# A transformer block on one core: values of twelve heads by seven products of halves, ahead of the attention

## The chip, the core and the metric

The kernel runs on one core of a Trainium2 chip. The metric is the device time of one execution in microseconds (us): the median of the runs, 2047.81 us for the kernel before (three runs, 2047.67 to 2048.41).

## The reference

One residual block over 512 positions of width 2048, all in float32:

```python
h = rmsnorm(x, g_attn)
proj = h @ w_in                      # columns: qa ka va | qf kf vf | f (8 gates)
o_sb  = stick_breaking_attention(qa, ka, va)       # 8 heads of 128
log_f = log_sigmoid(f + b_f)
o_fox = forgetting_attention(qf, kf, vf, log_f)    # 8 heads; z + c[t] - c[s], c = cumsum(log_f)
x = x + concat(headnorm(o_sb), headnorm(o_fox)) @ w_out
u = relu(rmsnorm(x) @ w_up)
x = x + (u * u) @ w_down
y = rmsnorm(x)
```

The change touches the projection of the values (va, vf), the row of c that the forgetting heads add to their scores, the preparation of w_out, and the norm of a head's output.

## The kernel before

**Precision.** Each float32 operand is split into a high part (a cast to a rounded format, on ScalarE, L71 or L74) and a low part (the difference, on VectorE, L72 or L75). A product is three matmuls, high x high, high x low, low x high (`mm3`, L103 to L106). So every chunk of weights that comes in by DMA (`load_w`, L88, tile `wraw`, three buffers) costs a cast and a subtraction of its size before TensorE can use it (tiles `wh`, `wl`, three buffers, `hi_lo`, L80).

**Order.** Loops are unrolled, and a planner orders the instructions of each engine ahead of time, by program order as priority, by estimated durations and by free buffers; `tc.high_priority()` lifts the attention of a head above the rest, and `tc.issue_after(ins)` keeps instructions on the engine of `ins` behind it. Each engine then takes its own list strictly in that order; loads and stores go through SP's list.

**First stage** (L348 to L369). x arrives in blocks, is transposed on TensorE (L179), multiplied by g_attn and split into hH, hL (16 tiles of 128 x 512, kept until the last projection). In the same loop the values of the first pair of heads and the 8 gate columns (264 columns) are accumulated for four row blocks of 128 (`accumulate_v`, L182): the activations are the stationary operand, the weights move. The squares of x (L366, ScalarE) give the row factors r1 (`row_rstd`), which scale everything projected.

**Attention** (L450 to L475). Heads go in pairs, n = 0, 2, ... 14: the forgetting heads 6, 7, 0 to 5 first, then the eight stick-breaking heads. For a pair:

- `project` (L451) makes four projections q, k of 16 steps x 3 matmuls of 512 columns (accumulator `accq`), then `qf` (L221) and its split into u tiles, one buffer for each of the pair's four.
- For n < 8, two calls of `sums_of_weights` (L429): for one pair of row blocks of w_out, four differences of quarters (L439 to L442), splits of parts of them, and stores to DRAM (`wsums`, `whigh`, `wraws`), for seven products of halves in the output projection later.
- For n = 2, 6, 10, `accumulate_v` over 512 columns makes the values of four heads, this pair's and the next's: 16 steps x 4 row blocks x 3 matmuls (`accv`); n = 14 does 256 columns. `take_v` (L204) scales by r1 and splits into vh, vl.
- `attend_sb` (L288) or `attend_fox` (L304): scores, then exponentials, sums and masks on ScalarE, VectorE and POOL in the tile `w`, then `weigh` (L246): transposes of `w` (L251) into PSUM, split into `ph`, `pl`, matmuls with vh, vl into `o`, and the norm: squares (L277), their column sums by a matmul with ones (L282, L283), VectorE's mean plus epsilon (L284), logarithm and exponential (L110, L111), three VectorE steps (L112 to L114) and the scaled output in `mixed` (L286). `w`, `ph`, `pl` and the PSUM tile of scores have one buffer each, and the norm's intermediates live in `ph`, `pl`.
- A forgetting head gets its row of -c by a matmul of a selector with ckT (`ck`, L306), copied by ScalarE (`cb`, L308).

The rest, output projection and the two matrices of the MLP, already works with seven products of halves and is the same text after the change.

Of the kernel before, what the change touches and what calls it, by code (L numbers as in the profile page):

```python
# [8 lines left out]
F32 = mybir.dt.float32  # L9
# [17 lines left out]
NU = DFF // P // 2  # L27

# [7 lines left out]
def block_kernel(ctx, tc, x, g_attn, w_in, b_f, g_out_sb, g_out_fox, w_out, g_mlp, w_up, w_down, g_final, y):  # L36
# [10 lines left out]
    cp.tile([P, 96], F32, name="pad0")  # L47
    pad = ctx.enter_context(tc.tile_pool(name="pad", bufs=1, side="right"))
    pad.tile([P, 120], F32, name="pad2")
    mixp_cm = tc.tile_pool(name="mix", bufs=1, side="right", reuse_waits="tile")  # L50
    mixp = mixp_cm.__enter__()
    mixed = mixp.tile([P, 2 * NH, NT], F32, name="mixed")
    up_cm = tc.tile_pool(name="u", bufs=1, side="right", reuse_waits="tile")
    up = up_cm.__enter__()
# [70 lines left out]
    def along_free(trp, r, wide):  # L125

        for t in range(TB):
            dve.tensor_copy(wide[:, t * P:(t + 1) * P], r[:, t:t + 1].to_broadcast([P, P]))
        ps = trp.tile([P, NT], F32, tag="tr", name="trb")
        for t in range(TB):  # L130
            pe.transpose(ps[:, t * P:(t + 1) * P], wide[:, t * P:(t + 1) * P], ident)
        return ps
# [13 lines left out]
    cp.tile([P, 16], F32, name="pad1")  # L146
# [7 lines left out]
    wsums = dp.tile([P, NH // 2, 4, 2, 2, NT], F32, name="wsums")  # L154
    whigh = dp.tile([P, NH // 2, 2, NT], F32, name="whigh")
# [9 lines left out]

    with tc.tile_pool(name="att", bufs=1, side="right", reuse_waits="tile") as at:
# [3 lines left out]
        h4 = [[form1.tile([P, 4, NT], F32R, tag=EARLY[2 * i + j], name=f"h{c}{i}") for j, c in enumerate("HL")] for i in range(KC // 4)]  # L170
        hH, hL = ([h4[k // 4][c][:, k % 4, :] for k in range(KC)] for c in range(2))
        xq = x.rearrange("(t p) c -> p t c", p=P)

        def transpose_x(k, trp):

            c, i = divmod(k, 4)
            ps = trp.tile([P, NT], F32, tag="tr", name="tr")
            for t in range(TB):
                pe.transpose(ps[:, t * P:(t + 1) * P], mixed[:, 4 * c + t, i * P:(i + 1) * P], ident)  # L179
            return split(hH[k], hL[k], ps, g_in[:, k:k + 1])  # L180

        def accumulate_v(c0, m, steps, prepare=None, more=None, pool_=None):  # L182

            per = NT // m
            banks = [(acc if pool_ is None else pool_).tile([P, NT], F32, tag="acc", name="accv")
                     for _ in range(2 if more is not None else TB // per)]
            if more is not None:
                banks += [more.tile([P, NT], F32, tag="more", name="accm") for _ in range(2)]
            ps = [banks[t // per][:, t % per * m:(t % per + 1) * m] for t in range(TB)]
            k1 = 0  # L190
            for step in steps:
                k0, k1 = k1, k1 + step
                if prepare is not None:
                    prepare(k0, step)
                w = load_w([w_in[k0 * P:(k0 + step) * P, c:c + m // len(c0)].rearrange("(a p) c -> p a c", p=P) for c in c0],
                           step, m)
# [7 lines left out]
        def take_v(ps, pairs=1):  # L204
            vs = [tuple(at.tile([P, TB, 2 * P], F32R, tag=f"v{c}", name=f"v{c}", bufs=3) for c in "hl") for _ in range(pairs)]
            for t in range(TB):
                for i, (vh, vl) in enumerate(vs):
                    split(vh[:, t, :], vl[:, t, :], ps[t][:, i * 2 * P:(i + 1) * 2 * P], r1[:, t:t + 1])
                    last_heads[2] = lows[0]
            return vs  # L210

        def project_q(c0, c, rb):
# [8 lines left out]
            dve.tensor_tensor(f, ps, rb, op=ALU.mult)  # L221
# [24 lines left out]
        def weigh(h, v, hc, w, gv, left=2):  # L246
# [23 lines left out]
            if left == 1:  # L270
                n1 = at.tile([P, 2 * NT], F32, tag="vh", name="n1", bufs=3)
                n2 = at.tile([P, 2 * NT], F32R, tag="vl", name="n2", bufs=3)
# [11 lines left out]
            dve.tensor_scalar(va, q, 1.0 / P, EPS, op0=ALU.mult, op1=ALU.add)  # L284
            rsqrt(va, va, ra, sq)
# [18 lines left out]
        def attend_fox(h, v, hc, q, k):  # L304
            ck = atp.tile([P, NT], F32, tag="o", name="ck")
            pe.matmul(ck, nsel[:, h, :], ckT, start=True, stop=True)  # L306
            cb = at.tile([P, NT], F32, tag="ul5", name="cb")
            act.copy(cb, ck)  # L308
# [17 lines left out]
        o0 = 3 * WSB  # L326
        order = [NH + h for h in (6, 7, 0, 1, 2, 3, 4, 5)] + list(range(NH))

        def v_columns(h):
            return 2 * WSB + h * P if h < NH else o0 + 2 * WSB + (h - NH) * P  # L330

        with tc.tile_pool(name="tr0", bufs=2, space=PSUM) as trp:
            def columns(out, v, n):
                ps = trp.tile([P, NT], F32, tag="tr", name="trg")
                pe.transpose(ps[:, :n], v, ident[:n, :n])
                dve.tensor_copy(out, ps[:, :n])

            def column_vectors(out, *rows):
                n = sum(r.shape[0] for r in rows)
                v = at.tile([n, P], F32, tag="rows", name="rows")  # L340
                i = 0
                for r in rows:
                    act.dma_start(v[i:i + r.shape[0], :], r)
                    i += r.shape[0]
                columns(out, v, n)
# [1014 lines left out]
```

## Time and profile before

| | |
|---|---|
| median of three runs | 2047.81 us |
| span of the profiled execution, first to last instruction | 2045.7 us |
| instructions | 26813 |
| TensorE (PE) busy | 2030.4 us, 99% |
| VectorE (DVE) busy | 1666.6 us, 81% |
| ScalarE (ACT) busy | 1093.2 us, 53% |
| data moved by DMA | 402.40 MB, 197 GB/s |

The profile shows one execution; its own time outside the span is not listed, and the median of the runs is 2.1 us above the span. Engines: PE is TensorE's matmuls, PEld its weight loads, which overlap them; SP issues DMAs. L104 is line 104 of the kernel before. In a group's row, `out<-in` names the tiles, then come partitions x elements, the count, busy us and mean ns, and idle time ahead of it with what ended that. A timeline row has start, length, engine, line and tiles. A row of waits has the waiting group, what it waited for, us in total, times and the longest.

### The profile page before, as it was taken

What the parts mean: (1) busy time and instruction counts of PE and PEld (TensorE: products, weight loads), DVE (VectorE), ACT (ScalarE), POOL (GpSimd) and SP (SyncE); (2) the same over time, 40 slices, a digit from 0 to 9 for tenths busy, and PEclk for the clock granted to TensorE, in tenths of its full rate; (3) what the DMA queues carried; (4) which work ended last, traced back from release to release, by engine and by line L of the source; (5) the groups of instructions that cost most, each with busy time, mean ns of one, the idle gap of its engine ahead of it and who ended that gap; (6) DMA issues with size and microseconds to landing.
All of it is one profiled execution on the core that took longest, in us unless ns stands there. A gap on an engine that the chain in (4) does not pass through costs nothing.

```text
span 2045.7 us, 26813 instructions
## 1 busy us (share of the span) xinstructions
PE 2030.4 (99%) x10322; PEld 1734.8 (85%) x10322; DVE 1666.6 (81%) x1892; ACT 1093.2 (53%) x1578; POOL 57.5 (3%) x76
## 2 busy tenths in 40 slices
PE   9999999999999999999999999999999999999998
PEld 8888888888888888988888888888888888888887
DVE  5667755566577678899999999999799898898896
ACT  6434433445455566677677676776644434444344
POOL 0000000000010000000000000000000000000004
PEclk9999999999999999999999999999999999999999
DMA  7888743232328882656666667667685674674642
GB/s 249 295 284 271 251 131 86 73 93 75 80 74 276 283 275 91 219 175 193 210 193 215 196 198 220 188 208 257 223 296 211 218 253 178 235 253 172 224 160 87
DMA packets 258848, 402.40 MB, mean 197 GB/s; under 512 B 9456, under 2 KB 154912, under 8 KB 251168
## 3 DMA queue, kind: packets, MB, share of 16 engines
q1 hardware_dynamic: 257760, 398.56, 59.4%
q10 hardware_dynamic: 960, 2.13, 0.3%
q8 instruction: 81, 1.33, 0.3%
q14 instruction: 47, 0.39, 0.1%
HBM read 307.85 MB, written 92.80 MB: 196 GB/s over the span
## 4 chain that ended last, share of the span: by engine, by line
PE 94%; DVE 4%; ACT 1%; issue 1%; DMA 1%; POOL 0%; SPq 0%; ACTq 0%; DVEq 0%
PE psa L594 10%; PE accd L104 8%; PE accd L105 8%; PE accd L106 8%; PE accq L104 6%; PE accq L105 6%; PE accq L106 6%; PE psa L596 5%; PE psc L594 5%; PE psc L596 3%; PE psb L594 3%; PE accv L104 2%; PE accv L105 2%; PE accv L106 2%; PE m L104 1%; PE m L105 1%
## 5 line engine op out<-in xcount | busy, mean ns | idle before, releaser
L1172 ACT CAST wh<-wd 128x1024 fp32r<-128x1024 f32 x126 | 124.9, 999 | 167.7 <-PE accd L106 54.4
L1062 DVE TENSOR_TENSOR wl<-wu,wh 128x1024 fp32r<-128x1024 f32 x157 | 191.4, 1220 | 15.3 <-ACT wh L1056 15.3
L104 PE MATMUL accq<-hH,wh 128*128 128x512 f32 x512 | 200.4, 391 | 0.4 <-DVE vl L75 0.4
L105 PE MATMUL accq<-hL,wh 128*128 128x512 f32 x512 | 200.2, 391 | 0.0
L106 PE MATMUL accq<-hH,wl 128*128 128x512 f32 x512 | 200.2, 391 | 0.0
L594 PE MATMUL psa<-f,wh 128*128 128x512 f32 x728 | 182.4, 392 | 0.3 <-ACT l L628 0.3
L1056 ACT CAST wh<-wu 128x1024 fp32r<-128x1024 f32 x157 | 166.2, 1058 | 28.5 <-issue 11.3
L105 PE MATMUL accd<-wl,uf 128*128 128x512 f32 x436 | 169.6, 389 | 0.0
L106 PE MATMUL accd<-wh,uf 128*128 128x512 f32 x436 | 169.6, 389 | 0.0
L104 PE MATMUL accd<-wh,uf 128*128 128x512 f32 x436 | 169.5, 389 | 0.0
L72 DVE TENSOR_TENSOR wl<-wraw,wh 128x1024 fp32r<-128x1024 f32 (+2 forms) x101 | 119.0, 1179 | 57.8 <-ACT wh L71 52.2
L71 ACT CAST wh<-wraw 128x1024 fp32r<-128x1024 f32 (+2 forms) x101 | 101.8, 1009 | 111.6 <-PE accq L105 68.6
L1179 DVE TENSOR_TENSOR wl<-wd,wh 128x1024 fp32r<-128x1024 f32 x126 | 143.9, 1151 | 13.2 <-ACT wh L1172 12.7
L594 PEld LDWEIGHTS psa<-f,wh 128*128 128x128 f32 x728 | 131.0, 189 | 24.0 <-ACT l L628 0.5
L946 DVE TENSOR_TENSOR m<-m,accd 128x1024 f32<-128x1024 f32 x84 | 102.2, 1216 | 46.7 <-PE accd L106 46.7
L1172 ACT CAST wx<-wd 128x1024 fp32r<-128x1024 f32 (+1 forms) x82 | 80.8, 995 | 109.3 <-PE accd L106 43.0
L104 PEld LDWEIGHTS accq<-hH,wh 128*128 128x128 f32 x512 | 96.1, 188 | 20.2 <-PE accv L106 0.8
L106 PEld LDWEIGHTS accq<-hH,wl 128*128 128x128 f32 x512 | 96.2, 188 | 19.3
L105 PEld LDWEIGHTS accq<-hL,wh 128*128 128x128 f32 x512 | 96.2, 188 | 19.3
L104 PE MATMUL accd<-wx,uf 128*128 128x512 f32 x284 | 110.5, 389 | 0.0
L105 PE MATMUL accd<-wx,uf 128*128 128x512 f32 x284 | 110.5, 389 | 0.0
L106 PE MATMUL accd<-wx,uf 128*128 128x512 f32 x284 | 110.5, 389 | 0.0
(375 smaller groups left out, 4930.1 us busy)
## 6 DMA issues: line engine op xcount, KB each, us to landing
wu<-in_w_up_dram SPq DMA_DIRECT2D x60, 1024.0 KB, 6.6
ufd<-st SPq DMA_DIRECT2D x98, 512.0 KB, 4.1
wd<-in_w_down_dram SPq DMA_DIRECT2D x48, 1024.0 KB, 7.6
wraw<-in_w_in_dram SPq DMA_DIRECT2D x84, 512.0 KB, 3.8
uf<-ufd SPq DMA_DIRECT2D x42, 1024.0 KB, 7.2
mixed<-in_w_out_dram SPq DMA_DIRECT2D x8, 2048.0 KB, 7.7
wsums<-mixed SPq DMA_DIRECT2D x8, 2048.0 KB, 7.3
wo<-wsums SPq DMA_DIRECT2D x28, 512.0 KB, 5.0
```

Of the source, the lines that this page charges most:

```text
L71: ins = act.copy(hi, src)
L72: lows[0] = dve.tensor_tensor(lo, src, hi.bitcast(F32), op=ALU.subtract)
L104: pe.matmul(out, sh, mh, start=first, stop=False, skip_group_check=True)
L105: pe.matmul(out, sh, ml, start=False, stop=False, skip_group_check=True)
L106: return pe.matmul(out, sl, mh, start=False, stop=last, skip_group_check=True)
L594: pe.matmul(ps, hi[:, a, :], f_both(p, a), start=a == PAIRS[0] and p in (1, 5), stop=False, skip_group_check=True)
L596: ins = pe.matmul(ps[:, 2 * P:], lo[:, a, :], f_parts(p, a)[0], start=False, stop=a == PAIRS[-1], skip_group_check=True)
L946: dve.tensor_tensor(M[p][:, :, db, :], M[p][:, :, db, :], ps, op=ALU.add)
L1056: act.copy(rooms[k][0], srcs[k])
L1062: lows[0] = dve.tensor_tensor(lo, srcs.pop(k), hi.bitcast(F32), op=ALU.subtract)
L1172: act.copy(rooms[k + 3][0], srcs[k + 3])
L1179: dve.tensor_tensor(rooms[k + 2][1], srcs.pop(k + 2), rooms[k + 2][0].bitcast(F32), op=ALU.subtract)
```

## The change

1. **Values.** Before the attention, a stage of its own makes the values of the first seven pairs. The first pair and the gates are accumulated as before (with x's blocks k and k + 8 side by side). The other twelve heads are two groups of six (768 columns). For each group the activations (512 rows x 2048) and the weights (2048 x 768) are cut into halves both ways, and the four products of quarters, eight multiplications, become seven of sums and differences (the Winograd form): each 8 steps x 2 row blocks x 3 matmuls of 384 columns. The sums on the activations' side (x11, x21, x12, f5, and the splits in `make_left`) are made once, those on the weights' side per group, in place. Results are scaled by r1, added on VectorE, and stored to DRAM (`vd`); each pair loads its values back and splits them (`load_v`). The last pair is done as before.
2. **Sums of output weights.** One whole call per pair for n = 0 to 6; the other four are cut into halves of columns, three such pieces for each of n = 8, 10 and two for n = 12: seven pairs of heads instead of four.
3. **Gate rows.** c is transposed, negated, stored to DRAM (`ckd`), and each forgetting head loads its row broadcast over the partitions, instead of the selector matmul and the copy.
4. **Norm of a head.** The logarithm reads the sums from PSUM with scale and epsilon (a column `eps`); VectorE's step L284 goes, and L112 to L114 change their constants.
5. **Scale.** rbq, the row factors times 1/sqrt(128), goes; the query's multiply has the scale in it.

```diff
+        def v_product(p, b, ps, first):
+            b11, b12, b21, b22 = b
+            out, x_, y_ = {1: (b11, None, None), 2: (b21, None, None), 3: (b22, None, None), 5: (b11, b12, b11),
+                           6: (b11, b22, b11), 4: (b21, b21, b11), 7: (b12, b22, b12)}[p]
+            for a in range(0, K8, 2):
+                s_ = slice(a, a + 2)
+                if x_ is not None:
+                    dve.tensor_tensor(out[:, s_], x_[:, s_], y_[:, s_], op=ALU.subtract)
+                hi, lo = (w.rearrange("p (a b) -> p a b", a=2) for w in hi_lo(2 * NV))
+                split(hi, lo, out[:, s_])
+                for t in range(2):
+                    ts = slice(t * P, (t + 1) * P)
+                    for i in range(2):
+                        lh, ll = left(p, a + i)
+                        mm3(ps[t][:, :NV], lh[:, ts], ll[:, ts], hi[:, i, :], lo[:, i, :], first and a + i == 0, a + i == K8 - 1)
...
+        for group in (1, 2):
+            c0 = v_columns(order[2 if group == 1 else 8])
+            if group == 2:
+                b21 = quadrant(0, 1, 0, c0)
+            b = quadrant(1, 0, 0, c0), quadrant(2, 0, 1, c0), b21, quadrant(3, 1, 1, c0)
+            X = banks(accs[0])
+            v_product(2, b, X, True)
+            s0 = stored(0)
+            saved(s0, X, 0)
+            if group == 1:
+                make_left(5)
+            Y = banks(accs[1])
+            v_product(1, b, Y, True)
+            added(s0, Y, 0, 0)
...
+        def load_v(n):
+            group, i = [(0, 0), (1, 0), (1, 1), (1, 2), (2, 0), (2, 1), (2, 2)][n // 2]
+            raw = at.tile([P, TB, 2 * P], F32, tag="vr", name="vr")
+            sp.dma_start(raw, vd[group][:, :, i * 2 * P:(i + 1) * 2 * P])
+            vh, vl = v_tiles()
+            split(vh, vl, raw)
+            return vh, vl
...
-            dve.tensor_scalar(va, q, 1.0 / P, EPS, op0=ALU.mult, op1=ALU.add)
-            rsqrt(va, va, ra, sq)
+            act.activation(ra, q, AF.Ln, scale=1.0 / P, bias=eps)
+            act.activation(ra, ra, AF.Exp, scale=-0.5)
+            dve.scalar_tensor_tensor(sq, q, P * EPS, ra, op0=ALU.add, op1=ALU.mult)
+            dve.tensor_tensor(sq, sq, ra, op=ALU.mult)
+            dve.scalar_tensor_tensor(va, sq, -3.0 * P, ra, op0=ALU.add, op1=ALU.mult)
...
-            ck = atp.tile([P, NT], F32, tag="o", name="ck")
-            pe.matmul(ck, nsel[:, h, :], ckT, start=True, stop=True)
             cb = at.tile([P, NT], F32, tag="ul5", name="cb")
-            act.copy(cb, ck)
+            sp.dma_start(cb, ckd[h:h + 1, :].to_broadcast([P, NT]))
...
+                v = load_v(n) if n < 2 * NH - 2 else None
                 qk = [project(0), project(1)]
                 if n < NH:
-                    sums_of_weights(n)
-                    sums_of_weights(n + 1)
-
-                if n == 2 * NH - 2:
-                    ps = accumulate_v([v_columns(order[n])], 2 * P, [4] * 4, pool_=accs[1])
+                    sums_of_weights(n // 2, (0, 1), mixed[:, :NH].rearrange("p (q a) n -> p q (a n)", a=2))
+                else:
+                    for _ in range(3):
+                        if sums_late:
+                            m, d = sums_late.pop(0)
+                            sums_of_weights(m, (d,), at.tile([P, 4, NT], F32, tag="ws", name="ws"))
+                if v is None:
+                    ps = accumulate_v(v_columns(order[n]), 2 * P, 4, accs[1])
                     with tc.high_priority():
-                        vs = take_v(ps)
-                elif n % 4 == 2:
-                    c = [v_columns(order[n + i]) for i in (0, 2)]
-                    vs = take_v(accumulate_v(c[:1] if c[1] == c[0] + 2 * P else c, 4 * P, [2] * 8), 2)
-                v = vs.pop(0)
+                        v = take_v(ps)
```

After the part shown, a group goes on with product 5 (banks Z), 6 (added into Y), 4 (X), 7 (into Y) and 3 (into Z), with the remaining left forms made in the first group between them.

More of the change, by code (lines that the diff above doesn't have):

```diff
@@ L27 @@
 NU = DFF // P // 2
+NV = 3 * P
 OFF_Q = [896, 1024, 512, 0]
@@ L386, in block_kernel @@
[L386 to L401 removed]
+            fl = gates
@@ L404, in block_kernel @@
             fe = at.tile([P, TB, NH], F32, name="fe")
-            for t in range(TB):
-                dve.scalar_tensor_tensor(fl[:, t, :], ps[t][:, 2 * P:], r1[:, t:t + 1], bf, op0=ALU.mult, op1=ALU.add)
-            vs = take_v(ps)
             act.activation(fe, fl, AF.Abs)
```

330 lines of the change are left out of this document (208 added, 122 removed).

## Prediction, made before the changed kernel was run

> **What bounds the kernel now.** I read the page first, for who is busy and how the chain that ended last is made up.
>
> ```profile
> span 2045.7 us, 26813 instructions
> ...
> PE 2030.4 (99%) x10322; PEld 1734.8 (85%) x10322; DVE 1666.6 (81%) x1892; ACT 1093.2 (53%) x1578; POOL 57.5 (3%) x76
> ...
> PE   9999999999999999999999999999999999999998
> ...
> DVE  5667755566577678899999999999799898898896
> ...
> PEclk9999999999999999999999999999999999999999
> ...
> PE 94%; DVE 4%; ACT 1%; issue 1%; DMA 1%; POOL 0%; SPq 0%; ACTq 0%; DVEq 0%
> ```
>
> TensorE is busy in every slice, at full clock, and makes 94% of the chain. A busy row alone may hide gaps, so I read next what TensorE waited for, over the whole span.
>
> ```profile
> PE trg L335 <- POOL chl L400: 3.3, 1, 3.3
> PE tr L179 <- DVE wl L72: 1.0, 1, 1.0
> ...
> PE psa L594 <- ACT l L628: 0.3, 1, 0.3
> ```
>
> Apart from the start, no wait reaches 1.1 us. The kernel runs at the pace at which TensorE accepts matmuls, and the price of a matmul is the distance between two starts, not its recorded length (0.39 us, which overlaps the next). The timeline of TensorE gives the distances.
>
> ```profile
> 61.19 0.39 PE L105 MATMUL accq<-hL,wh 128*128 128x512 f32 x1
> ...
> 63.68 0.39 PE L104 MATMUL accq<-hH,wh 128*128 128x512 f32 x1
> ...
> 68.94 0.33 PE L104 MATMUL s<-uh 128*128 128x384 f32 x1
> 69.11 0.34 PE L105 MATMUL s<-ul,uh 128*128 128x384 f32 x1
> 69.28 0.34 PE L106 MATMUL s<-uh,ul 128*128 128x384 f32 x1
> 69.46 0.23 PE L104 MATMUL s<-uh 128*128 128x128 f32 x1
> ```
>
> Between the first two rows lie 11 steps of 512 columns: 2.49/11 = 0.2264 us each. Three of 384 columns take 69.46 - 68.94 = 0.52 us, 0.1733 each. So columns are what is paid for, with a small fixed part.
>
> **The change part by part.** *Values.* What is removed, and the gate matmul that goes with it:
>
> ```profile
> L105 PE MATMUL accv<-wl,hH 128*128 128x512 f32 x192 | 75.1, 391 | 0.0
> L106 PE MATMUL accv<-wh,hL 128*128 128x512 f32 x192 | 74.9, 391 | 0.0
> L104 PE MATMUL accv<-wh,hH 128*128 128x512 f32 x192 | 74.9, 391 | 0.0
> ...
> L306 PE MATMUL ck<-ckT,nsel x8: 389/389/389, 75.6 to 373.3; 128*128 128x512 f32 x8
> ```
>
> The twelve heads cost 3 x 192 = 576 matmuls of 512 columns: 576 x 0.2264 = 130.4 us. After, each group of six heads is 7 products x 8 chunks of rows x 2 row blocks x 3 terms = 336 matmuls of 384 columns, 672 for both: 672 x 0.1733 = 116.5 us. Gain 13.9 us. The first pair (264 columns) and the last (256) keep their matmuls. *Gate rows*: eight matmuls of 512 columns go, 8 x 0.2264 = 1.8 us; their ScalarE copy goes too. The rest (shorter transposes of the gates, scale folded into the query's multiply) is under 0.3 us and I put it at zero. Gross: 13.9 + 1.8 = **15.7 us**, the largest gain possible, since no wait of TensorE is there to be removed.
>
> *What the products ask of VectorE.* The trace has no 768-wide split, but its neighbours, and two adjacent instructions that show the pace:
>
> ```profile
> L72 DVE TENSOR_TENSOR wl<-wraw,wh 128x1024 fp32r<-128x1024 f32 x92 | 113.2, 1231 | 53.0 <-ACT wh L71 47.4 <-issue 5.5
> L72 DVE TENSOR_TENSOR ul<-qf,uh 128x512 fp32r<-128x512 f32 x32 | 22.7, 710 | 5.4 <-ACT uh L71 5.4
> L75 DVE SCALAR_TENSOR_TENSOR vl<-accv,r1v,vh 128x256 fp32r<-128x256 f32 x30 | 13.2, 475 | 5.5 <-ACT vh L74 5.4
> ...
> 445.18 1.21 DVE L72 TENSOR_TENSOR wl<-wraw,wh 128x1024 fp32r<-128x1024 f32 x1
> 446.31 1.00 DVE L113 TENSOR_TENSOR ph<-ph,ra 128x512 f32<-128x512 f32 x1
> ```
>
> Back to back, 1024 elements take 446.31 - 445.18 = 1.13 us. A 768-wide one lies between 0.71 and 1.23 us; halfway is 0.97, less 0.1 of overlap 0.87. One group has 28 low halves and 16 differences of weights: 44 x 0.87 = 38.3 us. The first group also has 8 low halves of left forms and 6 differences at 1.13 (15.8 us), and both have 8 sums out of PSUM at about 0.6 (between 0.475 at 256 and 0.71 at 512), 4.8 us. First group: 58.9 us of VectorE beside 336 x 0.1733 = 58.2 us of TensorE; second: 43.1. So the first group has no slack; the three weight buffers let VectorE run a quarter to three quarters of a product ahead. I take 1.5 us of TensorE idle there (0 if differences made in the stage before hide it, 6 if none are).
>
> *Entry.* The first product goes to free banks, the second needs a bank that waits for the row factors, and these wait for the last squares:
>
> ```profile
> 39.45 0.28 PE L106 MATMUL accv<-wh,hL 128*128 128x264 f32 x1
> ...
> 40.53 0.28 PE L106 MATMUL accm<-wh,hL 128*128 128x264 f32 x1
> ...
> 41.91 1.05 ACT L366 ACTIVATE ph<-mixed 128x1024 f32<-128x1024 f32 x1
> ...
> 46.77 1.06 ACT L366 ACTIVATE ph<-mixed 128x1024 f32<-128x1024 f32 x1
> ...
> 53.08 0.16 DVE L114 SCALAR_TENSOR_TENSOR r1v<-r1b,r1a 128x4 f32<-128x4 f32 x1
> ```
>
> From the last square's end (47.8) to the factors (53.2) pass 5.4 us. Four squares back to back need 4 x 1.2 = 4.8, and eight small evacuations about 2: 12 us. TensorE has 24 matmuls of the last chunks (9 steps in 1.08 us: 0.12 each, 2.9 us) and one product (8.3 us): 11.2 us. The wait is short by itself; but the first product's casts are queued behind those squares on ScalarE, and projections, which today fill this hole, have no banks until the products end. I take 3 us (0 to 6).
>
> *Moved into the attention.* Values are read back from DRAM: one 1 MB load and a 128x1024 split (1.13 us of VectorE) per pair, early enough. Gate rows come by eight broadcast loads on SP, ahead of whose queue stand weights; three weight buffers cover 24 x 0.2264 = 5.4 us each, so a late one costs nothing unless it blocks SP for about 10 us. Sums of weights: the same work, one whole instead of two per pair of heads at first, three halves per pair later. What bears load today without a wait:
>
> ```profile
> 66.70:101.20 34.50, 34.50 (x164) 28.89 (x163) 22.89 (x34) 14.05 (x24) 1.81 (x2) 1.00 0.90 306
> 101.20:145.00 43.80, 43.80 (x207) 36.75 (x206) 36.16 (x49) 19.06 (x31) 1.26 (x2) 1.00 0.78 274
> ...
> 397.20:613.20 216.00, 216.00 (x1088) 184.59 (x1087) 137.60 (x157) 105.48 (x126) 18.55 (x28) 1.00 0.29 79
> ```
>
> Columns: length, busy PE, PEld, DVE, ACT, POOL, clock, DMA share, GB/s. With DMA at 0.90, or VectorE at 36.16/43.8 = 83%, TensorE still had no gap. In the late heads VectorE is at 137.6/216 = 64%; without the value matmuls and with eight half sums (four differences at 0.6 us each, four of them with three more splits: about 26 us over three pairs) it comes to some 80%. I take 2.5 us of waits in the attention and 1 us where it begins (0 to 15 together; the rival below gives the upper end).
>
> Sum: -15.7 + 3 + 1.5 + 1 + 2.5 = -7.7. The profiled span is 2045.7 us, the median of the runs 2047.81; I keep the 2.1 us around the span: 2045.7 - 7.7 + 2.1 = **2040.1, rounded to 2040**. With no wait at all 2047.8 - 15.7 = 2032.1; with the upper ends of entry and group 2047.8 - 15.7 + 6 + 6 + 3.5 = 2047.6.
>
> **The rivals.** *1. The heads' own ring binds.* The value matmuls fill TensorE while a head passes through ScalarE and VectorE. The weights of a head (ph, pl) have one buffer, held until the head is normalised:
>
> ```profile
> 422.89 1.49 DVE L72 TENSOR_TENSOR pl<-pt,ph 128x1280 fp32r<-128x1280 f32 x1 [1.35 <-ACT ph L71]
> ...
> 448.64 0.75 DVE L286 SCALAR_TENSOR_TENSOR mixed<-os,g_rest,ph 128x512 f32<-128x512 f32 x1
> ...
> 452.47 1.49 DVE L72 TENSOR_TENSOR pl<-pt,ph 128x1280 fp32r<-128x1280 f32 x1 [1.18 <-ACT ph L71]
> ...
> 609.85 1.49 DVE L72 TENSOR_TENSOR pl<-pt,ph 128x1280 fp32r<-128x1280 f32 x1 [1.35 <-ACT ph L71]
> ```
>
> The next head's pl follows the normalisation by 4 us, and six such intervals take 609.85 - 422.89 = 187 us, 31.1 each. After the change a head has two projections, 96 x 0.2264 = 21.7 us, and its own scores and values (12 matmuls of 512 to 128 columns each, about 1.9 us), ten transposes and two sums, by the same steps about 5.5 us: 27.2. If 31.1 were the ring's own length, six intervals would be late by 6 x 3.9 = 23 us; the last pair's values (192 matmuls of 256 columns at about 0.12, 23 us), done while waiting, take back some 10 to 12 of it: gain 15.7 - 5.5 - 11, about 2048.5. Against it: TensorE never waited in these intervals, so 31.1 is what TensorE had to do, not the ring's length; and the change takes a step out of the ring:
>
> ```profile
> L284 DVE TENSOR_SCALAR ph<-ssq 128x512 f32<-128x512 f32 x14 | 9.6, 682 | 8.1 <-PE ssq L283 8.1
> ...
> L110 ACT ACTIVATE ra<-ph 128x512 f32<-128x512 f32 x14 | 8.8, 626 | 21.3 <-DVE ph L284 21.3
> ```
>
> L284 goes, for which ScalarE stood idle 21.3 us in 14 heads, 1.5 each. *2. Slower: half sums stretch that ring.* They stand in VectorE's strict order: 26/6 = 4.4 us per late head. Where all of it lies in the ring, 31.1 - 1.5 + 4.4 = 34.0 against rival 1's 31.1: six times 2.9 more, 2048.5 + 17 = 2066. It makes the kernel slower (over 2051.9) once a head takes more than about 31.7. Against it: sums aren't urgent, and attention is put ahead of them where the order is planned.
>
> *3. Weight loads set the pace.* The products load weights 672 times for 576.
>
> ```profile
> L104 PEld LDWEIGHTS s<-uh 128*128 128x128 f32 x64 | 12.1, 189 | 1.2
> ```
>
> If 0.189 us were a floor, 672 x 0.189 = 127.0, a gain of 3.4 for 13.9, and with it 2050.5. But 384-wide matmuls with new weights each start 0.1733 apart: loads overlap. The Trainium skill (TensorE: Matmul & The Clock Gate, Back-to-back issue gap) says that spacing in a stream is set by load and matmul together, about 81 ns at 128 columns and 131 at 512; an estimate along that line gives 114 ns at 384, so 76.6 us for 75.5, no gain at all. The trace disagrees: 226 ns at 512, 173 at 384.
>
> **How the numbers follow.** Forecast, with waits of 3 to 12 us in all, 2035 to 2044: 0.50. Waits under 3 us, 2032 to 2035: 0.14. Rival 1 or a long entry, 2044 to 2052: 0.19. Rival 2: 0.14. Rival 3: 0.03. A measurement tells 0.2% (4.1 us) from no change, so faster means under 2043.7 (0.64), same up to 2051.9 (0.21), slower beyond (0.15). The range goes from 2031.5 (the floor, 2032.1, and half a microsecond at the start) to 2050; it leaves out rival 2 and part of 1 and 3, under 2 in 10.
>
> **What would show it.** Right: 672 matmuls of 384 columns about 0.173 apart, none of ck, TensorE's waits over 1 us only at the entry to the products, in the first group and a few in the late heads, 5 to 11 us in sum. Wrong: steps of 0.19 between 384-wide matmuls (rival 3); idle TensorE before scores or transposes late in the attention with pl over 30 us apart (rivals 1 and 2, the second if the wait is for VectorE with sums ahead); a stall of over 6 us at the entry.

## The result, and the profile after the change

The changed kernel takes **2081.59 us** (median of four runs, 2080.97 to 2082.69) beside 2048.01 us for the kernel before in the same session (2047.67 to 2048.41): a ratio of **1.0167, 95% interval 1.0155 to 1.0179**. It is slower by some 33.6 us, where 8 us of gain were forecast. The profiled execution's span is 2081.0 us, 35.3 us above the 2045.7 of before.

From the page of the changed kernel: the engines' totals, the slices of TensorE, VectorE and the clock, and the shares of the chain that ended last.

```profile
span 2081.0 us, 27247 instructions
...
PE 2030.2 (98%) x10410; PEld 1749.6 (84%) x10410; DVE 1733.1 (83%) x1979; ACT 1128.2 (54%) x1623; POOL 53.1 (3%) x73
...
PE   7799999999997999999999999999999999999998
...
DVE  5875787776576667899999999999799899898896
...
PEclk9999999999998999999999999999999999999999
...
PE 85%; DVE 6%; DMA 4%; ACT 2%; issue 1%; SPq 0%; POOL 0%; ACTq 0%; DVEq 0%; POOLq 0%
```

The row of TensorE, all nines before up to its last slice, has 77 in its first two slices of 52 us and a 7 in the thirteenth (624 to 676 us); there the clock has an 8. TensorE's share of the chain fell from 94% to 85%. From slice fourteen on, the output projection and the MLP look as before. The busy time of TensorE alone (2030.2 us for 2030.4) says nothing: matmuls at half rate count as busy. The stretches of the attention and what stands ahead of it show it, first of the changed kernel, then of the kernel before. Columns: stretch, length, then busy us of PE, PEld, DVE, ACT and POOL (instructions in brackets), granted clock, DMA share, GB/s.

```profile
0.00:80.00 80.00, 59.65 (x362) 55.51 (x363) 56.33 (x85) 49.61 (x85) 0.73 (x7) 0.91 0.49 166
80.00:300.00 220.00, 218.52 (x1143) 198.33 (x1142) 165.28 (x225) 99.11 (x150) 4.62 (x11) 1.00 0.62 208
300.00:500.00 200.00, 195.59 (x930) 161.96 (x929) 149.31 (x224) 94.90 (x148) 8.81 (x16) 1.00 0.66 206
500.00:600.00 100.00, 100.00 (x483) 84.59 (x482) 62.59 (x68) 46.77 (x55) 8.92 (x12) 1.00 0.31 81
600.00:700.00 100.00, 85.01 (x482) 75.10 (x482) 69.83 (x88) 52.46 (x73) 8.44 (x12) 0.90 0.45 158
```

```profile
0.00:80.00 80.00, 75.49 (x453) 67.95 (x454) 49.17 (x79) 43.55 (x75) 4.74 (x13) 1.00 0.78 259
...
300.00:500.00 200.00, 199.62 (x952) 167.91 (x951) 114.30 (x151) 88.67 (x125) 12.16 (x18) 1.00 0.31 81
...
600.00:700.00 100.00, 98.95 (x552) 85.54 (x551) 75.32 (x93) 54.09 (x81) 3.23 (x6) 1.00 0.75 245
```

Busy time still hides gaps shorter than a recorded matmul (0.39 us, where the next starts after 0.227) and half rate. So I also summed, over all matmuls, how far the distance to the next start exceeds the usual one for its width (0.227 us at 512 columns, 0.173 at 384, 0.120 at 264 and 256, 0.109 at 128; excesses over 5%). I call this sum the **loss** of a stretch; it is worked out from the trace, in us:

| stretch | before | after | more |
|---|---|---|---|
| 0 to 80 | 6.3 | 28.9 | 22.6 |
| 80 to 300 | 1.8 | 3.9 | 2.1 |
| 300 to 500 | 2.1 | 8.9 | 6.8 |
| 500 to 600 | 0.7 | 0.7 | 0.0 |
| 600 to 700 | 2.6 | 21.3 | 18.7 |
| from 700 | 2.5 | 2.6 | 0.1 |

Together 50.3 us more; less the 15.7 us of matmuls saved this is 34.6, beside 35.3 measured. So the saving is real, and three holes swallow it three times over. The first has two parts: by the same sum 8.7 of its 22.6 us lie between 12 and 45 us, in the first stage, and 13.6 from 45 us on, at the entry to the products. What TensorE waited for in the holes, from the changed kernel's rows of waits:

```profile
PE accacc L101 <- DVE gates L281: 7.7, 1, 7.7
PE pt L450 <- POOL w L442: 7.3, 1, 7.3
PE accacc L101 <- ACT hH L71: 4.3, 6, 2.0
...
PE s L101 <- DVE pl L69: 2.4, 1, 2.4
```

The longest wait stands at the entry: product 1 (the second to be made) needs banks that hold the first pair's values and gates. TensorE's timeline there (start, length):

```profile
66.76 0.66 PE L101 MATMUL accacc<-wh,hH 128*128 128x384 f32 x1 [7.67 <-DVE gates L281]
67.22 0.52 PE L102 MATMUL accacc<-wl,hH 128*128 128x384 f32 x1
67.54 0.52 PE L103 MATMUL accacc<-wh,hL 128*128 128x384 f32 x1
...
72.86 0.33 PE L102 MATMUL accacc<-wl,hH 128*128 128x384 f32 x1
73.03 0.34 PE L103 MATMUL accacc<-wh,hL 128*128 128x384 f32 x1
```

Two things are to be seen: the idle 7.67 us, and that the 18 matmuls behind it start 0.32 us apart, then 0.17. Between 66.7 and 72.6 us the granted clock is 0.50. So the wait costs its own length and again some 2.6 us of half rate. VectorE's timeline shows why the gates were late:

```profile
61.18 0.16 DVE L111 SCALAR_TENSOR_TENSOR r1v<-r1b,r1a 128x4 f32<-128x4 f32 x1
...
66.39 0.22 DVE L281 SCALAR_TENSOR_TENSOR gates<-accacc,r1v,bf 128x8 f32<-128x8 f32 x1
```

The factors were there at 61.34; five us of differences and low halves stand between them and the first gates. From the start of the last four squares (48.19) to the end of the first gates (66.61) pass 18.4 us. The other wait over 7 us is the last head's, in three rows of the timeline:

```profile
647.74 0.80 PE L101 MATMUL s<-uh 128*128 128x512 f32 x1 [2.43 <-DVE pl L69]
...
666.75 2.39 PE L450 MATMUL pt<-ident,w 128*128 128x128 f32 x10 [7.30 <-POOL w L442]
...
683.80 0.75 DVE L488 SCALAR_TENSOR_TENSOR mixed<-os_last,g_rest,ph 128x512 f32<-128x512 f32 x1
```

From this head's scores to its transposes pass 19 us (17 in the kernel before), to its output 36, and TensorE had little else left to do: within the 19 us only 13 matmuls of the head before it, which weigh its values and sum its squares. Before, the last scores started at 613, and 90 matmuls of the last pair's values and over 70 of the output projection ran beside that head.

### The profile page after: what moved, and what is told of

Same layout as the page of the kernel before. It is cut to its first block, busy times and chain, and to the rows that moved or that the text cites. A ratio compares the mean times of both kernels' runs of the same rounds, so it can differ in the third digit from the quotient of the medians.

```text
span 2081.0 us, 27247 instructions
## 1 busy us (share of the span) xinstructions
PE 2030.2 (98%) x10410; PEld 1749.6 (84%) x10410; DVE 1733.1 (83%) x1979; ACT 1128.2 (54%) x1623; POOL 53.1 (3%) x73
## 4 chain that ended last, share of the span: by engine, by line
PE 85%; DVE 6%; DMA 4%; ACT 2%; issue 1%; SPq 0%; POOL 0%; ACTq 0%; DVEq 0%; POOLq 0%
PE psa L733 10%; PE accd L102 8%; PE accd L103 8%; PE accd L101 8%; PE psa L735 5%; PE psc L733 5%; PE accq L103 4%; PE accq L102 4%; PE accq L101 4%; PE psc L735 3%; PE psb L733 2%; PE m L102 1%; PE m L101 1%; PE m L103 1%; PE psb L735 1%; PE accacc L101 1%
## 5 line engine op out<-in xcount | busy, mean ns | idle before, releaser
L68 ACT CAST wh<-wraw 128x1024 fp32r<-128x1024 f32 (+2 forms) x77 | 76.4, 993 | 58.2 <-PE accq L102 48.1
L735 PEld LDWEIGHTS psa<-f,wl 128*128 128x128 f32 x728 | 99.4, 191 | 7.1
```

The source lines that it names most:

```text
L68: ins = act.copy(hi, src)
L735: ins = pe.matmul(ps[:, 2 * P:], lo[:, a, :], f_parts(p, a)[0], start=False, stop=a == PAIRS[-1], skip_group_check=True)
```

## The experiments

All are edits of the changed kernel, except one. Each time is beside a run of the kernel before on the same chip: 2047.49 us for the first four, then 2048.72, 2048.14, 2047.61 (four each) and 2047.98 (the last two). Single runs but for the last two, which were timed in three rounds. The runs of one kernel lay up to 4.8 us apart, so small differences between single runs say little.

**Row factors first.** Theory A was that the entry's loss is the late place of factors and gates in VectorE's order.

```diff
+            with tc.high_priority():
                 r1 = row_rstd(ss1, "r1")
+        with tc.high_priority():
             for t in range(TB):   # first_v, gates
```

> Row factors, evacuation of the first pair and gates are put ahead of the other work in the planner's order; nothing else. Theory A (at the entry the second product waits for banks that wait for row factors and gates queued behind differences and splits on VectorE): the 7.7 us wait before the second product falls under 2 us and the half-rate matmuls after it (2.7 us) go: 2071 to 2074 us. Rival (VectorE's total work in the first group is the bound): the wait moves to the splits of the weights, under 4 us gained, 2078 or more.

2085.74 us; the wait for the gates is 6.1 us. The gates came only 0.4 us earlier, at 65.95 for 66.39: the priority hardly moved the planned order, so this settles nothing about A.

**Ring freed.** Rival 1 of the prediction, as theory B.

```diff
-            if left == 1:
+            if left >= 1:   # norm's intermediates in spare value buffers
```

> The norm's intermediates of every head but the last go to the free value buffers, so ph and pl are free after the value matmuls. Theory B (ph and pl held until the norm set about 30 us per head; TensorE runs ahead, uses up its other work and idles at the last heads): heads 28.5 us apart or less in the late half, TensorE's idle between 600 and 700 us falls from 19 us to under 8, total 2062 to 2070 us. Rivals (half sums on VectorE; length of the last heads' own chain): spacing and idle stay, 2077 or more.

2091.32 us; the loss from 600 to 700 is 21.1, and pl's in the late half are 30.0 us apart on average. The buffers of ph and pl aren't what binds: **theory B falls**.

**No late differences.** Rival 2.

```diff
+                if len(ds) == 2:
                     dve.tensor_tensor(b11, b12, b11, op=ALU.subtract)   # and three more
```

> The eight late half sums are stored without their four differences (these weights are then wrong, everything else as before), which takes about 20 us from VectorE in the late heads. Theory B: under 4 us gained, 2078 or more. Rival (half sums stretch the ring of the late heads): heads 2 to 3 us closer, 2062 to 2070 us.

2075.86 us, between the two forecasts: 5.7 us go with the differences of the half sums, 3.7 of them at the end (loss 17.6). Their splits and stores were still there.

**Late values in the attention.** The second group's six heads are accumulated in the attention again.

```diff
-        for group in (1, 2):
+        for group in (1,):
-                v = load_v(n) if n < 2 * NH - 2 else None
+                v = load_v(n) if n < NH else None
```

> Only the first group is made by seven products ahead; the values of heads 0 to 5 of stick-breaking are made pair by pair inside the attention again (256 columns: 3 x 192 x 0.12 = 69 us for 58 of products). Theory (value matmuls were the work that filled TensorE while heads pass): idle between 600 and 700 us falls under 6 us, so 11 us more work less 15 to 18 us of waits: 2074 to 2078 us. If the waits have nothing to do with that work: 2090 or more.

2076.56 us, and the end is healed. The stretch from 600 to 700 us of this run:

```profile
600.00:700.00 100.00, 99.46 (x562) 87.28 (x561) 71.13 (x90) 51.71 (x75) 4.64 (x8) 1.00 0.57 187
```

TensorE is busy 99.46 us where it was 85.01, at full clock. The value matmuls were what TensorE did while the last heads passed through the other engines.

**Raw copies; squares behind the casts.** Banks are released without the factors.

```diff
-            act.mul(first_v[:, t], ps[t][:, :2 * P], r1[:, t:t + 1])
+            act.copy(first_v[:, t], ps[t][:, :2 * P])   # scaled afterwards; gates likewise
```

> The first pair's values and gates are copied out of PSUM unscaled, ahead of the other work on their engines, and scaled by the row factors afterwards, so that the second product's banks no longer wait for the factors. Theory A (the 7.7 us wait for the gates and the half rate behind it come from the factors' late place in VectorE's order): that wait falls under 2 us, the matmuls behind it start 0.173 apart instead of 0.32, 8 to 11 us less: 2070 to 2074. Rival (VectorE's and ScalarE's whole work in the first 80 us is the bound, wherever the factors stand): the idle time moves to later waits for hH and wl, under 4 us gained, 2077.5 or more.

> As the raw copies, and in addition the squares of x stand on ScalarE behind the casts of the transposed blocks. Theory A: the waits for hH (4.3 us in the changed kernel) go as well, 3 to 5 us below the run with raw copies alone, 2066 to 2070. Rival: ScalarE's order costs nothing, the same time as with raw copies alone within 1.5 us.

2084.14 and 2088.60 us. The wait for the gates is gone, and others are there in its place:

```profile
PE accacc L102 <- DVE wl L69: 5.9, 4, 2.6
PE accmore L102 <- DVE wl L69: 5.2, 2, 4.1
```

TensorE now waits for low halves of weights; the loss up to 80 us is 25.1 for 28.9, and 7.0 for 3.9 from there to 300. VectorE is full there, in whatever order: **theory A falls**. With the squares moved too, the waits for hH fell only from 3.7 to 3.4 us; of that run's further 4.5 us the trace has 5.5 in the MLP, which the edit doesn't touch, and I can't explain them.

**Projections held.** Theory C: TensorE runs ahead of the heads (110 to 117 projection matmuls for a head that needs 96) and has none left at the end.

```diff
+                    with behind(after_):   # q: scores, k: transposes of the head two before
                         mm3(ps, *w[i], hH[k], hL[k], k == 0, k == KC - 1)
```

> The planned order is held back: the query projection of a head comes behind the scores of the head two before it, its key projection behind that head's transposes, and the last pair's values behind the transposes of head 13. No operation is added or taken away. Theory C (TensorE runs ahead of the heads, uses up the projections and the last pair's values, and stands idle in the last two heads for want of other work): idle time from 600 to 700 us falls from 19 us to under 6, 2062 to 2068. Rival (a head's chain through ScalarE and VectorE is itself longer than 27 us, so that the idle time is only spread out over the heads): 2077 or more.

> All three edits together: unscaled copies, squares behind the casts, projections held back. Theories A and C, if both hold, add up: 2081.6 less 12 to 15 less 14 to 19, 2047 to 2055. If the gains overlap or one theory falls, 2060 or more.

2095.90 and 2098.32 us, worse. One interval of the first run, from VectorE's and TensorE's timelines:

```profile
592.71 1.49 DVE L69 TENSOR_TENSOR pl<-pt,ph 128x1280 fp32r<-128x1280 f32 x1 [1.35 <-ACT ph L68]
```

```profile
600.63 0.39 PE L101 MATMUL s<-uh 128*128 128x512 f32 x1
```

pl was done at 594.2, and the next scores started 6.4 us later, behind 27 projection matmuls that the hold had put there. An engine that takes its list in order makes a chain wait for whatever is listed ahead.

**Tighter order; the same with the ring freed.** Only half a key projection (24 matmuls) may stand behind the transposes (theory D).

```diff
-project_q(e, 2 * i, SCALE, a), project_q(e + WSB, 2 * i + 1, None, b)
+project_q(e, 2 * i, SCALE, (a, a)), project_q(e + WSB, 2 * i + 1, None, (a, b))   # one per half
```

> As the run with projections held, but cut finer: behind a head's transposes only half a key projection (24 matmuls, 5.4 us) may stand on TensorE before the next scores, not 39 as there; the query projection and the other half stand behind the scores; the last pair's values are spread behind the scores and the transposes of head 14. Nothing is added or taken away. Theory D: a head needs 19 us from scores to transposes and 5.2 from there to the next scores, 24.3 in all (heads 14 and 15 of the changed kernel, where nothing else stands on TensorE), less than the 27.2 of TensorE's work for a head; the 30 us of the heads come from TensorE's order alone. Then heads 8 to 14 follow each other at 27 to 28 us and the time is 2058 to 2068. Rival D2 (ph and pl, held by the norm of the head before, bind once TensorE does not): 29 us or more, 2077 or more, and the next run differs. Rival D3 (the chain meets the projections' own work on VectorE and ScalarE): 2077 or more in both.

> As the tighter order, and in addition the norm's intermediates of heads 0 to 14 live in spare value buffers, so that ph and pl come free with the value matmuls. Theory D: within 4 us of the tighter order alone, 2056 to 2068. Rival D2: 10 us or more below the tighter order alone, 2055 to 2066. Rival D3: 2077 or more.

2080.73 and 2083.48 us. Two rows of TensorE's timeline and two stretches, of the first:

```profile
505.60 0.39 PE L101 MATMUL s<-uh 128*128 128x512 f32 x1
...
532.76 0.39 PE L101 MATMUL s<-uh 128*128 128x512 f32 x1
```

```profile
500.00:600.00 100.00, 100.00 (x487) 84.75 (x486) 66.55 (x74) 51.62 (x59) 7.83 (x14) 1.00 0.30 79
600.00:700.00 100.00, 86.02 (x493) 76.03 (x492) 67.97 (x87) 49.39 (x71) 9.12 (x10) 0.93 0.50 168
```

The heads follow each other at 27.16 us without idle time, as theory D has it, and 27.2 is what the prediction worked out for a head's own matmuls. Still, 14 us are idle at the end: the mechanism was right and the time forecast wrong. Heads can't be faster than their own TensorE work; the last one lacks other work.

**Left differences left out, or done by POOL.** Theory E: VectorE's work is the entry's bound.

```diff
-            dve.tensor_tensor(x21[:, a], x11[:, a], x21[:, a], op=ALU.subtract)   # six such
+            pool.tensor_tensor(x21[:, a], x11[:, a], x21[:, a], op=ALU.subtract)   # second run
```

> The run with raw copies, and without the six differences that make left forms of x (products 3, 6 and 7 then get wrong operands; two of their inputs are zeros from POOL), 6 x 1.22 = 7.3 us of VectorE's work between 55 and 76 us. Theory E (VectorE is the bound of the entry: it is busy without a gap from 60 to 80 us with raw copies): idle time and half rate between 40 and 100 us fall by 5 to 9 us, 2075 to 2079. Rival (ScalarE's casts or the loads of weights are): within 2 us of the run with raw copies, 2082 to 2086.

> As before with raw copies, the six differences of x done by POOL instead of VectorE. Theory E: if POOL takes 2.5 us for one or less and disturbs VectorE little, most of the gain of leaving them out, 2076 to 2081; if POOL is slower or takes VectorE's access to memory, product 6 waits and nothing is gained, 2084 or more.

2077.65 us, 6.5 below raw copies alone for 7.3 us of VectorE's work left out. But the loss between 40 and 100 us fell only from 15.0 to 11.7, where theory E had 5 to 9 us; most of the rest of the gain stands from 230 us on, where the edit changes nothing. VectorE's work is on the path at the entry, for about half of what was forecast. By POOL 2087.25. From the timelines of POOL and of VectorE in that run:

```profile
62.39 2.36 POOL L293 TENSOR_TENSOR f<-x,x 128x1024 f32<-128x1024 f32 x1
```

```profile
60.00 2.34 DVE L273 TENSOR_SCALAR g_rest<-g_rest 128x16 f32<-128x16 f32 x1
...
62.56 3.28 DVE L69 TENSOR_TENSOR s<-f,s 128x1024 fp32r<-128x1024 f32 x1
...
72.61 1.21 DVE L69 TENSOR_TENSOR s<-x,s 128x1024 fp32r<-128x1024 f32 x1
```

A difference takes POOL 2.36 us, and VectorE's own of the same size beside it takes 3.28 instead of 1.21. The small step of 16 columns, 0.17 us in the changed kernel, takes 2.34 beside the POOL difference ahead of this one (59.34 to 62.31).

**No products.** Values of all pairs in the attention, a pair at a time; the rest of the change stays.

```diff
-        for group in (1, 2):   # with the forms of x and all that belongs to the products
-                v = load_v(n) if n < 2 * NH - 2 else None
+                v = load_v(n) if n == 0 else None
```

> Without the stage of products: the values of every pair but the first are accumulated in the attention, a pair at a time over 256 columns, all other parts of the change as they are. By the steps of the traces six pairs cost 6 x 192 x 0.12 = 138 us where before the twelve heads cost 130.4, and the gate matmuls' 1.8 us stay saved: 2048 + 7.8 - 1.8 = 2054 if sums, gate rows, norm and scale cost nothing else, 2051 to 2058, with entry and end of the attention without idle time as before. 2062 or more if these parts cost time by themselves.

2076.94 us, 23 over the forecast. Its stretches:

```profile
0.00:80.00 80.00, 66.21 (x379) 58.77 (x380) 38.63 (x64) 40.38 (x68) 1.27 (x10) 0.89 0.74 246
...
300.00:500.00 200.00, 200.00 (x1215) 180.07 (x1215) 113.80 (x146) 85.60 (x113) 11.14 (x20) 1.00 0.33 89
...
600.00:700.00 100.00, 99.47 (x561) 87.36 (x560) 71.15 (x90) 50.97 (x74) 4.65 (x8) 1.00 0.59 192
```

This cuts the loss in two. With the values back in the attention the holes from 300 to 500 and at the end are gone (1.5 and 1.4 us); 7.9 us of loss stand between 230 and 300 instead. The entry's hole isn't gone: the loss up to 80 us is 21.8, though VectorE has 38.63 us of work there instead of 56.33. So it takes no product to lose 15.5 us more there than the kernel before. But it is not the same hole. Between 12 and 33 us, where the forms of x are not made in this run, the loss is 3.0 us, beside 7.6 in the changed kernel and 1.0 before. Behind that no projection filled the stage, since their weights were late, as SP's timeline shows:

```profile
27.10 0.37 SPq L91 DMA_DIRECT2D wraw<-in_w_in_dram  x1
42.60 0.82 SPq L477 DMA_DIRECT2D mixed<-in_w_out_dram  x2
43.53 2.21 SPq L91 DMA_DIRECT2D wraw<-in_w_in_dram  x2
```

SP's list stood for 15 us at a load into `mixed`, which takes the room of x's blocks and so has to wait for the last square of x (done at 42.58). The projections' weights are listed behind it, and the first projection started at 52.88.

**Projections at the entry; one head ahead; both.**

```diff
+            early_q() if group == 1 else None   # head 0's 48 + 48 matmuls, after products 2 and 1
```

```diff
+    # behind the scores of the head just before: three quarters of a head's projections
+    # behind the transposes of the head two before: the first quarter
+    # last pair's values: one quarter behind transposes 14, three behind scores 15
```

> Head 0's two projections (96 matmuls of 512 columns, 21.7 us, and 4.6 us of VectorE for them) stand between the first products instead of ahead of the first scores, product 2 goes to the transposes' banks, and the two differences for product 3 are made later. Theory E (VectorE's work is too dense for TensorE's at the entry): idle time and half rate from 40 to 130 us fall from 16 to under 6, 2069 to 2074. Rival (the waits follow VectorE's queue however much TensorE work stands beside it): 2078 or more.

> Three quarters of a head's projections (72 matmuls) stand behind the scores of the head just before it and one quarter behind the transposes of the head two before, so that the last projections stand beside head 14; of the last pair's values one quarter behind head 14's transposes and three behind head 15's scores. Nothing is added or taken away. Theory F (the loss at the end is TensorE's want of other work in the last head's chain of 40 us, since the projections are done one head too early): idle time from 600 to 700 us falls from 19 to under 7, 2063 to 2070. Rival (with less lead, projections reach their scores late, or the chain is stretched by the projections' splits): 2077 or more, with idle time spread over the heads.

> Projections at the entry and one head ahead, together. If theories E and F hold the gains add up: 2050 to 2060. If one falls, 2062 to 2074.

2097.47, 2072.70 and 2075.54 us. The first gave 5 us back at the entry and lost 14 more at the end (35.5): work done early is missing late. The second healed the end, as theory F says:

```profile
300.00:500.00 200.00, 191.88 (x917) 160.57 (x916) 148.80 (x227) 95.69 (x148) 13.53 (x17) 0.98 0.66 205
...
600.00:700.00 100.00, 99.27 (x562) 86.87 (x560) 72.41 (x90) 52.56 (x76) 4.71 (x8) 1.00 0.59 195
```

The loss at the end fell from 21.3 to 2.3, but 8.9 us of gain came out of it, not 19: some moved to 300 to 500 (13.7 for 8.9) and to 80 to 300 (8.3 for 3.9). Both together did not add up: 2075.54 us lies beyond both of its forecasts.

**Kernel before with projections held.** Theory G. In the kernel before, these matmuls ran between 33 and 58 us, by line:

```profile
L106 PE MATMUL accq<-hH,wl 128*128 128x512 f32 x28 | 11.0, 394 | 0.0
L104 PE MATMUL accq<-hH,wh 128*128 128x512 f32 x28 | 11.0, 393 | 0.0
L105 PE MATMUL accq<-hL,wh 128*128 128x512 f32 x28 | 10.9, 390 | 0.0
```

84 matmuls, 19 us at 0.2264. In the changed kernel the first projection starts at 181.0 us, behind the products.

```diff
+                    with tc.issue_after(turned_factors[0].ins):
                         mm3(ps, *w[i], hH[k], hL[k], k == 0, k == KC - 1)
```

> The kernel before, with every projection held on TensorE behind the transposes of the row factors; nothing is added or taken away. Theory G: the 84 projection matmuls that stood between 33 and 58 us leave TensorE idle there, 13 to 19 us more, 2060 to 2067. Rival (the loss at the changed kernel's entry comes from its other order of x's blocks, the forms of x and the squares, none of which is here): 2054 or less.

2072.44 us (2071.12 to 2073.16), a ratio of 1.0120 (1.0103 to 1.0136): the kernel before with nothing added loses 24 us. Its two longest waits and two stretches:

```profile
PE trb L133 <- DVE rw L130: 9.7, 1, 9.7
PE pt L254 <- POOL w L246: 7.8, 1, 7.8
```

```profile
0.00:80.00 80.00, 65.94 (x400) 59.76 (x401) 48.73 (x77) 42.22 (x74) 4.74 (x13) 0.94 0.76 252
...
600.00:700.00 100.00, 89.56 (x504) 78.87 (x503) 67.89 (x86) 48.42 (x71) 9.35 (x8) 0.93 0.55 186
```

Both holes of the changed kernel are there: 11.2 us more loss up to 80 us, while the row factors are made, and 11.7 more at the end, at the same transposes. TensorE's planned order changed with the hold, and only 37 matmuls of the last pair's values were left beside the last head, for 90 before.

**Projections in the first stage.**

```diff
+                if k == 5:
+                    early_chunk(0, 0)   # head 0's projections by quarters of the blocks
+                    early_chunk(1, 0)
```

> The changed kernel with projections one head ahead (as in the run of that name, scores ahead of the value matmuls of the head before), and with head 0's two projections (96 matmuls, 21.7 us) inside the first stage, half of them after x's blocks 5 and 13, half at its end; product 2 in the transposes' banks, unscaled copies. Theory G: idle time and half rate up to 130 us fall from 31 to under 14, and with the 9 us of the late projections the time is 2050 to 2059. Rival (ScalarE and VectorE are the bound of the first stage, so that more casts there stretch it): 2066 or more.

2069.17 us (2068.49 to 2073.26), a ratio of 1.0107 (1.0092 to 1.0122), the best version of the change here and still slower than before. Its stretches:

```profile
0.00:80.00 80.00, 69.07 (x415) 60.87 (x416) 51.00 (x82) 51.89 (x89) 0.73 (x7) 1.00 0.60 192
80.00:300.00 220.00, 208.37 (x1080) 188.76 (x1079) 164.55 (x225) 97.44 (x148) 8.18 (x11) 0.98 0.58 195
...
600.00:700.00 100.00, 99.27 (x560) 87.10 (x559) 72.60 (x90) 52.91 (x76) 4.61 (x8) 1.00 0.59 199
```

The loss up to 80 us is halved (14.2 for 28.9) and the end's is gone (1.9); 16.3 us came back between 80 and 300, most of it between 180 and 230 (12.9), where head 0 now has only head 1's projections beside its chain, and 3.6 between 300 and 500.

## Why the prediction was wrong, point by point

**The gross gain was right.** 384-wide products start 0.173 us apart, the gate matmuls are gone, and the balance of losses closes to 0.7 us with 15.7 us saved. Rival 3 falls. The first group's 1.5 us holds only from 80 us on, where the loss up to 300 grew by 2.1 in all, with no wait at the start of the attention. Ahead of that VectorE is busy without a gap from 58.8 to 72.6 us, so part of the hole at the entry belongs to this term: "the first group has no slack" was right, and its price was not.

**The step that failed first is the entry:** "TensorE has 24 matmuls of the last chunks ... and one product (8.3 us): 11.2 us. The wait is short by itself; ... I take 3 us (0 to 6)". Up to 80 us the loss grew by 22.6. Of these 13.6 stand where the term does, from 45 us on, beyond its upper end; the way from the last squares to the bank, worked out as 12 us, took 18.4, since the factors and gates stood in VectorE's list among the first group's differences and low halves. The other 8.7 stand in the first stage ahead of it, for which the sum has no term at all.

I named a cause, "projections, which today fill this hole, have no banks until the products end", and gave it no price. It had one in the trace of before: 84 matmuls, 19 us, between 33 and 58 us; I quoted rows of the same stretch for the squares and the value matmuls and passed over them. Two runs show that it counts, whatever keeps the projections away: taking just these matmuls out of that place in the kernel before costs 11.2 us there, nearly all behind 33 us, and putting 96 of them into the changed kernel's first stage takes the loss up to 80 us from 28.9 to 14.2 (25.1 with the unscaled copies alone, which that run has too). VectorE's work there counts too: 7.3 us of it left out took 3.3 us off the loss. How the 13.6 us divide between the two is open. The loss between 12 and 33 us is neither's: the kernel before has no projections there. It is 6.6 us more than before, and 2.0 more where the forms of x are not made, which points to these forms; no run took them out alone. The squares' place on ScalarE alone gained nothing.

**The second is the attention:** "I take 2.5 us of waits in the attention and 1 us where it begins (0 to 15 together; ...)". It measured 25.5 from 300 to 700 us, beyond the upper end. Two arguments carried it: that TensorE had no gap at 83% of VectorE, and that 31.1 us a head was TensorE's own work. Both are true, and neither prices what matters, the work that is left for the last head. Before, TensorE had 130 us of value matmuls to spread over the heads, which the change took out. After, a head has 27.2 us of TensorE's own work beside a chain of some 24, which leaves little over, and at the end 36 us of chain stand beside what was left of values and output projection.

**Rival 1** (2048.5) had the shortage and the wrong mechanism. The buffers of ph and pl aren't the bound: in the same six heads pl's follow each other at 29.2 us on average, not at 31.1, and freeing the buffers gained nothing, alone or in the tighter order. Its step "the last pair's values ..., done while waiting, take back some 10 to 12 of it" has the wrong sign: done early, they are missing beside the last head, and the run that kept them for it (one head ahead) lost only 2.3 us at the end. **Rival 2** (2066) foretold the side, with luck in that: leaving out the late sums' differences gave 5.7 us of its 17, so it is a small part.

Of its own signs two came, "a stall of over 6 us at the entry" and "idle TensorE before scores or transposes late in the attention". The second stood beside "pl over 30 us apart", and that pairing did not come: pl's were up to 31.0 us apart while TensorE was busy without a gap, and 24 to 28 where it stood idle.

So what was shown: the change takes away matmuls that TensorE did while other engines held the chain, projections at the first stage and values in the heads. With the values put back, the holes in the heads close (late values the end, no products the middle as well); with projections and the last values moved to where the chain is (one head ahead, in the first stage), the holes shrink, 12.4 us in all. What stays open: how the entry divides, and whether an order exists that closes all three holes at once; no run here beat the kernel before.

## What to carry to other kernels

Ahead of taking work from the busiest engine, list the chains through other engines that it covers, and for each what is left to run beside it, above all for the first and the last: saved matmuls count only where something else fills their place. An engine that is busy at 99% with one long queue says that the work is well placed, not that any work less is time less. A filler has a place as well as a size; done early it is gone late.

## What the runs showed of the hardware

- **Half rate after a wait.** Behind TensorE's wait of 7.67 us, 18 matmuls of 384 columns started 0.32 us apart instead of 0.173, and the granted clock there was 0.50. Behind a wait of 2.43 us (the last scores, with a wait of 1.31 us and little work ahead of it) and one of 9.7 us (kernel before with projections held) it was the same. The slow stretches were 2.6 to 6 us long.
- **POOL beside VectorE.** A 128x1024 difference with two operands in SBUF took POOL 2.36 us, and held VectorE's instruction of the same kind beside it to 3.28 us for 1.21. In that run VectorE began four differences of two SBUF operands while POOL was in one of its own; each ended 0.6 to 1.1 us after POOL's, about its own usual length (0.69 to 1.21), as if it had waited for POOL's end. Steps that read PSUM took their usual 0.47 us beside it.
